# A hybrid decoder layer: q, k and the MLP's input transposed by VectorE and DMA, and every projection with the activations as the stationary operand

## The chip, the cores and the metric

The kernel runs on one core of a Trainium2 chip. The metric is the device time of one execution in microseconds. TensorE is called PE, VectorE DVE, ScalarE ACT, GpSimd POOL and SyncE SP in the profile; SP does no arithmetic here and issues the transfers (DMAs).

## The reference

One decoder layer on 256 tokens of width 2048, all in float32:

```python
h = rmsnorm(x, ln1);  dq, dk, dv, sq, sk, sv = split(h @ w_in)      # six parts of 1024 columns
# group A, 8 heads: two 64-dim maps each, partial rotary on q and k
w = softmax(q1 k1^T / 8) - lam * softmax(q2 k2^T / 8)               # causal
diff = rmsnorm(w @ dv) * (1 - lam_init)
# group B, 8 heads of 128: stick-breaking attention
z = sq sk^T / sqrt(128)
a = exp(log_sigmoid(z) + reversed exclusive cumsum of log_sigmoid(-z))   # strictly causal
sb = rmsnorm(a @ sv)
x = x + concat(diff, sb) @ w_out
x = x + square(relu(rmsnorm(x, ln2) @ w_mlp_in)) @ w_mlp_out        # 8192 wide
out = rmsnorm(x, ln_f)
```

## The kernel before

Every large product is computed to float32 accuracy from float32r operands: each operand is split into a high part (`wh`, `a[:, 0]`) and a rest (`wl`, `a[:, 1]`), and three products (high x high, high x rest, rest x high) are added in PSUM. Weights come in chunks of 512 x 512 (1 MB, `issue_dma`, SP's queue, three buffers before the MLP and six in it). A chunk is two **jobs**; for each, `issue_conv` splits a tile of 128 x 1024: ACT makes `wh` (line 214), DVE makes `wl` by a subtraction (line 217). The conversions run three jobs ahead of the products (`AHEAD`), five in the MLP.

Two forms of product stand side by side. In `products_acc` (lines 248 to 261) the activations are stationary, the weights move, 512 columns at a time, and the result has tokens on partitions: a job has 2 contraction tiles x 2 token tiles x 3 products, 12 of 512 columns. In `products_T` (lines 264 to 288), used for sq and sk alone, the weights are stationary and the result comes out transposed, with features on partitions, as attention wants its q and k: a job has 8 products of 512 columns (high and rest of the activations side by side, line 271) and 8 of 256 columns (line 276).

What products_acc makes for q and k of the differential group (dq, dk) is transposed on PE against an identity matrix (line 425, 8 transposes of 128 x 128 per block of 512 columns, in two groups of four), and so is the MLP's input x after the output projection (line 643, four per pair of tiles). For sq and sk the scale 1/rms of each token has to lie along the columns: `x_norm` builds it with one product (line 363).

The MLP's hidden layer is already transposed in another way (`turn_task`): DVE transposes 32 x 32 blocks out of PSUM into `bl` (line 711), 16 DMAs of 32 KB, all issued by SP (line 716), move the blocks to their partitions in `hT`, DVE squares the ReLU (line 718), and ACT and DVE split the result into `aT` (lines 724, 725).

The work between the products hangs on **side tasks**: generators that advance by one step, up to the next `yield`, after each job (`tick`; the first two tasks of the queue get a step). `prep_task` makes q and k ready, `diff_task` and `sb_task` are the two attentions, one per group of four heads, and end in `mixT`, the eight pairs of tiles that the output projection reads; `x2_task` makes `xs2`, the MLP's input, from x after the output projection's column block. The order of the output jobs is written out: first the tiles that are ready early for column blocks 0 and 1 (12 jobs, from `n_proj` to `n_out0`), then the last chunk of both, then blocks 2 and 3. The MLP goes in four quarters of 2048 hidden columns: four `in_group`s, then four `out_group`s that read `aT` in the order in which it was made. Within these rules a planner orders the instructions of each engine when the program is built, by times of its own; each engine then takes them in that order.

Of the kernel before, what the change touches and what calls it, by code (L numbers as in the profile page):

```python
# [18 lines left out]
P = 128  # L19
# [6 lines left out]
CK = 4  # L26
# [18 lines left out]
def tile_hybrid_layer(  # L45
# [187 lines left out]
    def run_jobs(upto, nside=2):  # L233
        while state["job"] < upto:
            i = state["job"]
            if i in hooks:
                hooks[i]()
            while state["conv"] < min(i + 1 + state["ahead"], len(jobs)):
                issue_conv()
            c, h, products, after, _ = jobs[i]  # L240
            products(h, *sp.pop(i, (None, None)))
            if after is not None:
                after()
            tick(nside)
            state["job"] += 1


    def products_acc(get_acc, act, k0, first, last):
# [12 lines left out]
        return f  # L261


    def products_T(get_acc, act, k0, done):
        def f(h, wh, wl):
            acc = get_acc()
            last = k0 + (h + 1) * HK == KT

            def high(i, j):
                kt = k0 + h * HK + j  # L270
                nc.tensor.matmul(acc[i], wh[:, j, i * P:(i + 1) * P], act(kt).rearrange("p a s -> p (a s)"),  # L271
                                 start=kt == 0, stop=False, skip_group_check=True)

            def low(i, j):
                kt = k0 + h * HK + j
                state["mm"] = nc.tensor.matmul(acc[i][:, S:2 * S], wl[:, j, i * P:(i + 1) * P], act(kt)[:, 0, :],  # L276
                                               start=False, stop=kt == KT - 1, skip_group_check=True)


            tiles = range(NB // P)  # L280
            for part in ([(i,) for i in tiles] if last else [tiles]):
                for one in (high, low):
                    for i in part:
                        for j in range(HK):
                            one(i, j)
                if last:
                    done(part[0])
        return f
# [41 lines left out]
    rstd_row = {k: cpool.tile([P, S], F32, name=f"rstd_row_{k}") for k in ("sq", "sk")}  # L330
# [20 lines left out]
    def x_norm():  # L351
# [7 lines left out]
        dg = ap_.tile([P, NT, P], F32, tag="on", name="rstd_diag", bufs=1)  # L359
        for t in range(NT):  # L360
            nc.vector.tensor_scalar_mul(dg[:, t, :], ident, rstd1[:, t:t + 1])
        rp = ps_sc.tile([P, S], F32, tag="sc", name="rstd_row_ps")
        nc.tensor.matmul(rp, negone, dg.rearrange("p t s -> p (t s)"), start=True, stop=True)
        nc.vector.tensor_scalar_mul(rstd_row["sk"], rp, -1.0)
        nc.vector.tensor_scalar_mul(rstd_row["sq"], rp, -(128.0 ** -0.5))
# [33 lines left out]

    grp = {}  # L400

    def prep_task(kind):

        src = grp[kind, "src"]
        v = src.rearrange("p t (g c) -> p t g c", c=64)
# [12 lines left out]
        yield  # L418
        dst = ap_.tile([P, HG, S], F32, tag="qkT", name=f"T_{kind}", bufs=4)
        for hp in range(HG // 2):  # L420
            tp = ps_tp.tile([P, 2 * S], F32, tag="tp", name=f"tp_{kind}_{hp}")
            for hh in range(2):
                h = hp * 2 + hh
                for t in range(NT):
                    nc.tensor.transpose(tp[:, hh * S + t * P:hh * S + (t + 1) * P],
                                        src[:, t, h * P:(h + 1) * P], ident)
            yield
            nc.vector.tensor_copy(dst[:, hp * 2:hp * 2 + 2, :],
                                  tp.rearrange("p (h s) -> p h s", h=2))
        grp[kind] = dst  # L430
# [20 lines left out]
    def diff_task(gi):  # L451
# [4 lines left out]
        for h in range(HG):  # L456
# [16 lines left out]
            e = ap_.tile([P, 2, 3 * P], F32, tag="e", name=f"e_{nm}", bufs=3)  # L473
# [37 lines left out]
    def sb_task(gi):  # L511
# [4 lines left out]
        for hp in range(HG // 2):  # L516
# [12 lines left out]
            t = ap_.tile([P, 2, 3 * P], F32, tag="e", name=f"t_{nm}", bufs=3)  # L529
# [18 lines left out]
            a = ap_.tile([P, 2, 3 * P], F32, tag="e", name=f"a_{nm}", bufs=3)  # L548
# [15 lines left out]
    def proj_T_block(kind):  # L564

        c0 = cols[kind[:2]] + int(kind[2]) * NB
        acc = {}
        dst = {}

        def get_acc():  # L570
            if not acc:
                for i in range(HG):
                    acc[i] = ps_acc.tile([P, NB], F32, tag="acc", name=f"acc_{kind}{i}")
                dst[0] = ap_.tile([P, HG, S], F32, tag="qkT", name=f"T_{kind}", bufs=4)
            return acc

        def done(i):
            t1 = ap_.tile([P, S], F32, tag="t1", name=f"t1_{kind}{i}", bufs=1)
            nc.scalar.copy(t1, acc[i][:, S:2 * S])
            nc.vector.tensor_tensor(t1, acc[i][:, 0:S], t1, op=ALU.add)  # L580
            nc.vector.tensor_tensor(dst[0][:, i, :], t1, rstd_row[kind[:2]], op=ALU.mult)

        def after():
            grp[kind] = dst[0]
            if kind[1] == "k":
                side.append(sb_task(int(kind[2])))

        for c in range(KT // CK):
# [79 lines left out]
    for nb in (0, 1):  # L668
        out_chunk(nb, KT // CK - 1)
# [275 lines left out]
```

## Time and profile before

| | us |
|---|---|
| three runs | 1119.19, 1118.60, 1118.12 (median 1118.6) |
| profiled execution | 1118.63 |
| its span (first to last instruction) | 1116.9 |
| PE busy in the span | 1106.0 |
| DVE, ACT, POOL busy | 652.8, 512.4, 2.9 |

The span is what the profile shows; the time of an execution has 1.7 us beside it. A product's duration in the profile (389 ns for 512 columns) is from its start to the end of its drain; products overlap, so the price of one in a row of them is the distance of two starts, or its piece in the chain of waits.

### The profile page before, as it was taken

How to read it: one execution, taken by the hardware profiler on the slowest of the kernel's cores; microseconds unless marked ns; L12 is line 12 of the kernel's file. 1: busy time of each engine (PE TensorE's matmuls, PEld its weight loads, DVE VectorE, ACT ScalarE, POOL GpSimd, SP SyncE). 2: the span in 40 equal slices, each digit the busy share in tenths (PEclk: the TensorE clock that was granted, in tenths of full speed). 3: DMA queues.
4: the chain of work that ended last, by engine and by line, in shares of the span. 5: the costliest groups of instructions: out<-in, count | busy, mean ns of one | idle time of the engine just before them, and what ended most of it. 6: DMA issues, size and time to landing. Idle time of an engine off the chain costs nothing.

```text
span 1116.9 us, 13378 instructions
## 1 busy us (share of the span) xinstructions
PE 1106.0 (99%) x5213; PEld 919.6 (82%) x5213; DVE 652.8 (58%) x817; ACT 512.4 (46%) x665; POOL 2.9 (0%) x16
## 2 busy tenths in 40 slices
PE   9999999999999999999999999999999999999996
PEld 6887888888888888888888888888888888888886
DVE  5755756766555655665455565545556555555752
ACT  5645544655555644444333444434444433444541
POOL 1000000000000000000000000000000000000000
PEclk9999999999999999999999999999999999999999
DMA  8754554454545854766665576666557666565712
GB/s 287 227 171 153 170 175 144 152 187 149 177 165 212 321 183 137 263 226 206 211 198 162 182 261 225 201 197 198 184 182 251 221 195 195 198 210 180 263 39 76
DMA packets 125683, 216.02 MB, mean 193 GB/s; under 512 B 8210, under 2 KB 25652, under 8 KB 125492
## 3 DMA queue, kind: packets, MB, share of 16 engines
q1 hardware_dynamic: 125332, 214.65, 57.5%
q8 instruction: 41, 0.67, 0.2%
q10 hardware_dynamic: 288, 0.52, 0.1%
q14 instruction: 22, 0.18, 0.0%
HBM read 204.65 MB, written 2.10 MB: 185 GB/s over the span
## 4 chain that ended last, share of the span: by engine, by line
PE 99%; DMA 0%; DVE 0%; SPq 0%; ACT 0%; issue 0%; DVEq 0%; ACTq 0%
PE ia L260 10%; PE ia L259 10%; PE ia L258 10%; PE ma L258 10%; PE ma L259 10%; PE ma L260 10%; PE acc_sk L271 3%; PE acc_sq L271 3%; PE oacc L260 3%; PE oacc L258 3%; PE oacc L259 3%; PE acc_dq L258 1%; PE acc_sq L276 1%; PE acc_sk L276 1%; PE acc_dk L258 1%; PE acc_dq L260 1%
## 5 line engine op out<-in xcount | busy, mean ns | idle before, releaser
L217 DVE TENSOR_TENSOR wl<-w,wh 128x1024 fp32r<-128x1024 f32 (+1 forms) x385 | 469.3, 1222 | 382.2 <-ACT wh L214 380.8
L214 ACT CAST wh<-w 128x1024 fp32r<-128x1024 f32 (+1 forms) x385 | 402.5, 1049 | 497.3 <-PE ia L260 195.7
L258 PE MATMUL ia<-wh,xs 128*128 128x512 f32 x512 | 199.4, 389 | 0.0
L260 PE MATMUL ia<-wh,xs 128*128 128x512 f32 x512 | 199.3, 389 | 0.0
L259 PE MATMUL ia<-wl,xs 128*128 128x512 f32 x512 | 199.2, 389 | 0.0
L258 PE MATMUL ma<-wh,aT 128*128 128x512 f32 x480 | 186.7, 389 | 0.0
L259 PE MATMUL ma<-wl,aT 128*128 128x512 f32 x480 | 186.7, 389 | 0.0
L260 PE MATMUL ma<-wh,aT 128*128 128x512 f32 x480 | 185.4, 389 | 0.0
L258 PEld LDWEIGHTS ia<-wh,xs 128*128 128x128 f32 x512 | 96.1, 188 | 20.0
L259 PEld LDWEIGHTS ia<-wl,xs 128*128 128x128 f32 x512 | 96.1, 188 | 19.9
L260 PEld LDWEIGHTS ia<-wh,xs 128*128 128x128 f32 x512 | 96.1, 188 | 19.9
L258 PEld LDWEIGHTS ma<-wh,aT 128*128 128x128 f32 x480 | 90.1, 188 | 18.7
L260 PEld LDWEIGHTS ma<-wh,aT 128*128 128x128 f32 x480 | 90.1, 188 | 18.7
L259 PEld LDWEIGHTS ma<-wl,aT 128*128 128x128 f32 x480 | 90.1, 188 | 18.7
L258 PE MATMUL oacc<-wh,mixT 128*128 128x512 f32 x128 | 50.5, 394 | 0.0
L259 PE MATMUL oacc<-wl,mixT 128*128 128x512 f32 x128 | 50.1, 391 | 0.0
L260 PE MATMUL oacc<-wh,mixT 128*128 128x512 f32 x128 | 49.8, 393 | 0.0
L271 PE MATMUL acc_sk<-xs,wh 128*128 128x512 f32 x128 | 36.7, 399 | 0.0
L271 PE MATMUL acc_sq<-xs,wh 128*128 128x512 f32 x128 | 34.9, 397 | 0.0
L260 PEld LDWEIGHTS oacc<-wh,mixT 128*128 128x128 f32 x128 | 24.0, 188 | 4.9
L258 PEld LDWEIGHTS oacc<-wh,mixT 128*128 128x128 f32 x128 | 24.1, 188 | 4.8
L259 PEld LDWEIGHTS oacc<-wl,mixT 128*128 128x128 f32 x128 | 24.1, 188 | 4.8
(224 smaller groups left out, 1105.6 us busy)
## 6 DMA issues: line engine op xcount, KB each, us to landing
w<-in_w_mlp_in_dram SPq DMA_DIRECT2D x64, 1024.0 KB, 5.7
w<-in_w_mlp_out_dram SPq DMA_DIRECT2D x64, 1024.0 KB, 7.3
w<-in_w_in_dram SPq DMA_DIRECT2D x46, 1024.0 KB, 5.2
w<-in_w_out_dram SPq DMA_DIRECT2D x16, 1024.0 KB, 5.1
hT<-bl SPq DMA_DIRECT2D x256, 32.0 KB, 1.9
w<-in_w_in_dram SPq DMA_DIRECT2D x4, 512.0 KB, 7.8
x<-in_x_dram SPq DMA_DIRECT2D x3, 512.0 KB, 10.1
lnf_t<-in_ln_f_dram SPq DMA_DIRECT2D x1, 1024.0 KB, 6.5
```

The lines of the kernel that those rows point to most:

```text
L214: state["wh"] = nc.scalar.copy(wh[:, j], w[:, j])
L217: state["wl"] = nc.vector.tensor_tensor(wl[:, j], w[:, j], wh[:, j].bitcast(F32), op=ALU.subtract)
L258: nc.tensor.matmul(acc[t], a[:, 0, st], wh[:, j, :], start=s0, stop=False)
L259: nc.tensor.matmul(acc[t], a[:, 0, st], wl[:, j, :], start=False, stop=False)
L260: state["mm"] = nc.tensor.matmul(acc[t], a[:, 1, st], wh[:, j, :], start=False, stop=s1)
L271: nc.tensor.matmul(acc[i], wh[:, j, i * P:(i + 1) * P], act(kt).rearrange("p a s -> p (a s)"), start=kt == 0, stop=False, skip_group_check ...
L276: state["mm"] = nc.tensor.matmul(acc[i][:, S:2 * S], wl[:, j, i * P:(i + 1) * P], act(kt)[:, 0, :], start=False, stop=kt == KT - 1, skip_g ...
```

## The change

All six projections use `products_acc`; `products_T` and `proj_T_block` go. What is made with tokens on partitions (dq, dk, sq, sk, and the MLP's input x) is transposed as the MLP's hidden layer is, by a common function `turn`: two DVE transposes and 16 DMAs, which now alternate between SP's and GpSimd's queue (in the MLP's hidden layer too). For q and k the DMAs land in the tile that the projection wrote (`src`), and ACT copies from there to the order that attention reads. `prep_task` takes six steps where it took four, for sq and sk too. In the 12 output jobs before `n_out0` tasks get two steps each. One pair of output jobs is exchanged. The tag "e" (exponentials) has two buffers, no longer three.

```diff
@@ run_jobs
             tick(nside)
+            if n_proj <= i < n_out0:
+                tick(nside)
@@ products_T: removed
-                nc.tensor.matmul(acc[i], wh[:, j, i * P:(i + 1) * P], act(kt).rearrange("p a s -> p (a s)"),
-                                 start=kt == 0, stop=False, skip_group_check=True)
...
-                state["mm"] = nc.tensor.matmul(acc[i][:, S:2 * S], wl[:, j, i * P:(i + 1) * P], act(kt)[:, 0, :],
...
@@ x_norm
-        rp = ps_sc.tile([P, S], F32, tag="sc", name="rstd_row_ps")
-        nc.tensor.matmul(rp, negone, dg.rearrange("p t s -> p (t s)"), start=True, stop=True)
...
+        nc.vector.tensor_scalar_mul(rstd_sq, rstd1, 128.0 ** -0.5)
@@ new
+    def turn(dst, bl, src, engines):
+        for t in range(NT):
+            nc.vector.transpose(bl[:, t].rearrange("p f (k b) -> p f k b", b=32),
+                                src[t].rearrange("p (k f a) -> p f k a", k=4, f=4))
+        dv = dst.rearrange("p (t i) k b -> p t i (k b)", t=NT)
+        for i in range(4):
+            for f in range(4):
+                engines[(i * 4 + f) % len(engines)].dma_start(
+                    dv[f * 32:(f + 1) * 32, :, i, :], bl[i * 32:(i + 1) * 32, :, f, :])
@@ prep_task
+        if kind[0] == "d":
+            rotary(kind, src)
+        yield
+        bl = ap_.tile([P, NT, 4, 4 * 32], F32, tag="bl", name=f"bl_{kind}", bufs=1)
+        turned = src.rearrange("p t c -> p (t c)").rearrange("p (i k b) -> p i k b", k=HG, b=32)
+        turn(turned, bl, [src[:, t, :] for t in range(NT)], [nc.gpsimd, nc.sync])
+        for _ in range(4):
+            yield
+        dst = ap_.tile([P, HG, S], F32, tag="qkT", name=f"T_{kind}", bufs=4)
+        nc.scalar.copy(dst.rearrange("p k (i b) -> p k i b", b=32), turned.rearrange("p i k b -> p k i b"))
...
-                    nc.tensor.transpose(tp[:, hh * S + t * P:hh * S + (t + 1) * P],
-                                        src[:, t, h * P:(h + 1) * P], ident)
-            yield
-            nc.vector.tensor_copy(dst[:, hp * 2:hp * 2 + 2, :],
-                                  tp.rearrange("p (h s) -> p h s", h=2))
@@ diff_task, sb_task: three tiles of tag "e"
-            e = ap_.tile([P, 2, 3 * P], F32, tag="e", name=f"e_{nm}", bufs=3)
+            e = ap_.tile([P, 2, 3 * P], F32, tag="e", name=f"e_{nm}", bufs=2)
...
@@ proj_T_block: removed; proj_block appends prep_task for q and k of both groups, sb_task behind sk
-            nc.scalar.copy(t1, acc[i][:, S:2 * S])
-            nc.vector.tensor_tensor(t1, acc[i][:, 0:S], t1, op=ALU.add)
-            nc.vector.tensor_tensor(dst[0][:, i, :], t1, rstd_row[kind[:2]], op=ALU.mult)
...
@@ x2_task
+        turn(x2T, bl, [xt[nb][:, t, :] for t in range(NT)], [nc.sync, nc.gpsimd])
+        yield
+        yield
         for p2 in range(nb * 2, nb * 2 + 2):
-                    nc.tensor.transpose(tp[:, j * S + t * P:j * S + (t + 1) * P],
-                                        xt[nb][:, t, (kt % 4) * P:(kt % 4 + 1) * P], ident)
...
+                nc.scalar.activation(hi[j], x2T[:, :, k, :], AF.Copy, scale=g)
...
+                nc.vector.scalar_tensor_tensor(lo[j], x2T[:, :, k, :], g, hi[j].bitcast(F32),
+                                               op0=ALU.mult, op1=ALU.subtract)
+            yield
@@ output jobs
+    jobs[n_out0 + 1], jobs[n_out0 + 2] = jobs[n_out0 + 2], jobs[n_out0 + 1]
@@ turn_task of the MLP
-                    nc.sync.dma_start(hv[f * 32:(f + 1) * 32, :, i, :], bl[i * 32:(i + 1) * 32, :, f, :])
+            turn(hT, bl, [acc[t] for t in range(NT)], [nc.sync, nc.gpsimd])
```

## Rows read from the trace of the kernel before

**Rows 1.** The page's first part: busy us, share of the span, instructions of each engine.
```profile
PE 1106.0 (99%) x5213; PEld 919.6 (82%) x5213; DVE 652.8 (58%) x817; ACT 512.4 (46%) x665; POOL 2.9 (0%) x16
```
**Rows 2.** The page's second part: granted clock of PE, tenths, in 40 slices.
```profile
PEclk9999999999999999999999999999999999999999
```
**Rows 3.** The waits of PE: total us, times, longest; the first of three.
```profile
PE warm_a L321 <- DVE three_c L105: 1.3, 1, 1.3
```
**Rows 4.** The waits of all engines, the second longest in total.
```profile
ACT wh L214 <- PE ia L260: 195.7, 126, 1.9
```
**Rows 5.** The chain of waits between 157 and 289 us, shares by line.
```profile
by line: PE acc_sk L271 22.7%; PE acc_sq L271 22.5%; PE acc_sq L276 11.5%; PE acc_sk L276 11.5%; PE acc_sv L258 5.7%; PE acc_sv L260 5.5%; PE acc_sv L259 5.5%; PE sc_d L467 2.6%; PE sc_s L524 2.0%; PE o_d L508 2.0%; PE o_s L508 2.0%; PE wtp
```
**Rows 6.** The chain in order of time, 244 to 262 us: start, us, what.
```profile
247.57 1.84 PE acc_sq L271 x8
249.41 0.95 PE acc_sq L276 x8
```
**Rows 7.** Timeline of PE in the MLP: start, duration; 11 products stand between.
```profile
459.73 0.39 PE L258 MATMUL ia<-wh,xs 128*128 128x512 f32 x1
...
462.45 0.39 PE L258 MATMUL ia<-wh,xs 128*128 128x512 f32 x1
```
**Rows 8.** The chain in order of time, two stretches (48 to 75, 359 to 425 us).
```profile
49.32 0.43 PE rstd_row_ps L363 x2
...
64.99 0.44 PE tp_dk L425 x4
...
373.98 0.44 PE x2tp L643 x4
```
**Rows 9.** Groups of instructions by line: count, busy us, mean ns, idle before.
```profile
L217 DVE TENSOR_TENSOR wl<-w,wh 128x1024 fp32r<-128x1024 f32 (+1 forms) x385 | 469.3, 1222 | 382.2 <-ACT wh L214 380.8
...
L711 DVE STREAM_TRANSPOSE bl<-ia 128x512 f32<-128x512 f32 x32 | 20.9, 692 | 0.0
...
L580 DVE TENSOR_TENSOR t_sk<-acc_sk,t_sk 128x256 f32<-128x256 f32 x8 | 3.4, 420 | 1.5 <-ACT t_sk L579 1.5
...
L579 ACT COPY t_sq<-acc_sq 128x256 f32<-128x256 f32 x8 | 3.0, 375 | 3.4 <-DVE T_sq L581 1.5 <-PE acc_sq L271 1.0 <-PE acc_sq L276 0.8
...
L608 ACT ACTIVATE src_dk<-acc_dk,rstd 128x512 f32<-128x512 f32 x4 | 2.7, 689 | 2.8 <-PE acc_dk L260 2.7
```
**Rows 10.** Instructions on hT (ns min/median/max), and the page's DMA issues (us to landing).
```profile
L716 SPq DMA_DIRECT2D hT<-bl x256: 585/595/1825, 433.6 to 1031.2; - x128
...
hT<-bl SPq DMA_DIRECT2D x256, 32.0 KB, 1.9
```
**Rows 11.** Timeline of all engines at the end of the first quarter's last in_group.
```profile
498.90 10.92 SPq L716 DMA_DIRECT2D hT<-bl  x16
...
511.15 1.23 DVE L718 SCALAR_TENSOR_TENSOR hT<-hT 128x1024 f32<-128x1024 f32 x1
...
513.84 1.29 DVE L725 TENSOR_TENSOR aT<-hT,aT 128x512 fp32r<-128x512 f32 x2
...
514.59 0.39 PE L260 MATMUL ma<-wh,aT 128*128 128x512 f32 x1
```
**Rows 12.** The page's DMA issues: count, KB each, median us to landing.
```profile
w<-in_w_in_dram SPq DMA_DIRECT2D x46, 1024.0 KB, 5.2
```
**Rows 13.** Instructions on the weight tile w: SP's longest issue.
```profile
L195 SPq DMA_DIRECT2D w<-in_w_out_dram x16: 367/368/2333, 291.0 to 364.9; - x16
```
**Rows 14.** Timeline at the end of the output projection.
```profile
409.51 1.28 DVE L652 TENSOR_TENSOR x<-x,oacc 128x512 f32<-128x512 f32 x2
...
409.80 0.39 PE L258 MATMUL ia<-wh,xs 128*128 128x512 f32 x1
```
**Rows 15.** Chain and timeline around the second stick-breaking group.
```profile
288.60 0.23 PE acc_sk L276 x2
...
292.86 0.67 PE sc_s L524 x6
...
357.10 0.74 DVE L157 SCALAR_TENSOR_TENSOR mixT<-mtp_s,g2T,mixT 128x512 fp32r<-128x512 f32 x1
```

More of the change, by code (lines that the diff above doesn't have):

```diff
@@ L260, in f @@
                     state["mm"] = nc.tensor.matmul(acc[t], a[:, 1, st], wh[:, j, :], start=False, stop=s1)
[L261 to L270, printed above, removed]
-                nc.tensor.matmul(acc[i], wh[:, j, i * P:(i + 1) * P], act(kt).rearrange("p a s -> p (a s)"),
-                                 start=kt == 0, stop=False, skip_group_check=True)
-            def low(i, j):
-                kt = k0 + h * HK + j
-                state["mm"] = nc.tensor.matmul(acc[i][:, S:2 * S], wl[:, j, i * P:(i + 1) * P], act(kt)[:, 0, :],
[L277 to L287, printed above, removed]
         return f
@@ L329, in tile_hybrid_layer @@
     rstd_dq = cpool.tile([P, NT], F32, name="rstd_dq")
-    rstd_row = {k: cpool.tile([P, S], F32, name=f"rstd_row_{k}") for k in ("sq", "sk")}
+    rstd_sq = cpool.tile([P, NT], F32, name="rstd_sq")
     def sumsq(dst, src, name):
@@ L404, in prep_task, with rotary @@
         src = grp[kind, "src"]
+        if kind[0] == "d":
[8 more added lines that the diff above has]
+        nc.scalar.copy(dst.rearrange("p k (i b) -> p k i b", b=32), turned.rearrange("p i k b -> p k i b"))
+        grp[kind] = dst
+    def rotary(kind, src):
         v = src.rearrange("p t (g c) -> p t g c", c=64)
@@ L528, in sb_task @@
             z = sc[:, :, :3 * P]
-            t = ap_.tile([P, 2, 3 * P], F32, tag="e", name=f"t_{nm}", bufs=3)
+            t = ap_.tile([P, 2, 3 * P], F32, tag="e", name=f"t_{nm}", bufs=2)
             nc.scalar.activation(t, z, AF.Abs)
@@ L547, in sb_task @@
             yield
-            a = ap_.tile([P, 2, 3 * P], F32, tag="e", name=f"a_{nm}", bufs=3)
+            a = ap_.tile([P, 2, 3 * P], F32, tag="e", name=f"a_{nm}", bufs=2)
             nc.scalar.activation(a, z, AF.Exp)
@@ L562, in tile_hybrid_layer @@
     order = [f"{k}{g}" for g2 in ("d", "s") for g in range(2) for k in (g2 + "q", g2 + "k", g2 + "v")]
[L564 to L578, printed above, removed]
-            nc.scalar.copy(t1, acc[i][:, S:2 * S])
-            nc.vector.tensor_tensor(t1, acc[i][:, 0:S], t1, op=ALU.add)
-            nc.vector.tensor_tensor(dst[0][:, i, :], t1, rstd_row[kind[:2]], op=ALU.mult)
[L583 to L588, printed above, removed]
-            view = w_in[0, c * CK * P:(c + 1) * CK * P, c0:c0 + NB].rearrange("(k p) n -> p k n", p=P)
-            add_chunk(view, products_T(get_acc, act_xs, c * CK, done), after if c == KT // CK - 1 else None)
     def proj_block(kind):
@@ L605, in after @@
                            bufs=2)
-            sc_ = rstd_dq if kind[1] == "q" else rstd1
+            sc_ = {"dq": rstd_dq, "sq": rstd_sq}.get(kind[:2], rstd1)
             for t in range(NT):
@@ L613, in after @@
                 side.append(diff_task(int(kind[2])))
+            if kind[:2] == "sk":
+                side.append(sb_task(int(kind[2])))
         for c in range(KT // CK):
@@ L620, in tile_hybrid_layer @@
     for kind in order:
-        (proj_T_block if kind[:2] in ("sq", "sk") else proj_block)(kind)
+        proj_block(kind)
     n_proj = len(jobs)
```

32 lines of the change are left out of this document (8 added, 24 removed).

## The prediction, made before the change was run

> **What bounds the kernel now.** I read the engine totals first: the reader is to see PE at 99% of the span with no other engine over 58% [rows 1]. A busy PE could still be a slow one, so the clock row is next: the granted clock is in its top tenth in all 40 slices, the upper of its two levels (2.4 GHz), so nothing is to be won or lost by a faster clock [rows 2]. Then the waits of PE: three in the whole execution, 1.9 us together, all before 8 us, of which the longest is shown [rows 3]. PE therefore has its operands on time from beginning to end, and the span is a sum of PE instructions. The waits of the other engines say the same from their side: ScalarE's conversions of weights sit idle until PE gives a buffer back [rows 4]. So two questions decide: how many microseconds of PE work the change takes away, and whether the new route delivers every transposed tile before PE comes to it.
>
> **PE work that goes: the four sq and sk blocks.** Between 157 and 289 us the chain of waits is all PE, and its shares give the old form its price: 22.7 and 22.5% for the 512-column products, twice 11.5% for the 256-column ones, together 68.2% of 132 us, 90.0 us [rows 5]. In the undisturbed stretch one job of this form (8 and 8 products) is 1.84 + 0.95 = 2.79 us [rows 6]. The new form needs for the same job 12 products of 512 columns. In the MLP 12 such starts lie 462.45 - 459.73 = 2.72 us apart, 0.2267 us each [rows 7]. There are 4 blocks of 8 jobs, 384 products: 87.1 us. Saved 2.9 us by the totals, 32 x 0.07 = 2.2 us by the clean jobs; the totals also hold the jobs that attention work interrupts, and the new form will be interrupted too, so I take 2.8. The number of columns is the same in both forms; what goes is a per-instruction loss, 0.1186 us for 256 columns against half of 0.2267.
>
> **PE work that goes: transposes.** Four of them take 0.44 us of the chain, both for q and k and for the MLP's input [rows 8]. By the code q and k of the differential group lose 8 such groups, the MLP's input 8 more: 16 x 0.44 = 7.0 us. The product that spreads rstd over columns goes too: 0.43 us [rows 8]. Nothing is added on PE: sq and sk take the new route as well. Sum on PE: 2.8 + 7.0 + 0.4 = 10.2 us.
>
> **What VectorE and ScalarE get.** Twelve turns (8 of q and k, 4 of the MLP's input) cost two 128x512 transposes each, 0.69 us by the ones in the trace (these read PSUM, the new ones SBUF; I take the same): 16.6 us more. Eight 128x512 copies out of PSUM (at the same 0.69), 16 additions and 16 multiplications of 0.42 go from VectorE: 19 us less. ScalarE loses 16 copies of 0.375 (6.0 us), and gets 8 evictions of 0.69 and 8 copies of 128x1024, for which I take two evictions each: 10.6 us more [rows 9]. Both stay far below PE, and conversions run ahead of PE as far as the buffers go, so all this costs nothing as long as that cover of some jobs (2.72 us each) holds. The splits of the MLP's input keep their number. Fewer buffers for the exponentials (two for three) cost nothing either: within a task only two are alive. If two tasks collide, the softmax is late next, not PE.
>
> **What the queues get.** Each turn issues 16 transfers of 32 KB. SP issues one in 0.595 us and it lands 1.9 us after the issue began [rows 10]; a whole turn of the MLP takes SP 10.92 us, 0.68 each [rows 11]. The change adds 192 transfers and gives half of all 448 to GpSimd: SP goes from 256 to 224, and 5.5 us per turn instead of 10.9. In the projections this is new work in front of the weight loads: eight turns of 5.5 us. A chunk of weights lasts two jobs, 5.4 us, and there are three buffers: a load is issued when a buffer's second half is converted and its own first half is converted five jobs later, 13.6 us, of which it needs 5.2 to land [rows 12] and 5.5 for the turn: 2.9 us are left, and the conversions' lead of three jobs behind them. Nothing for this, 0 to 1 us per turn as the upper end.
>
> **The unknown: an issue by GpSimd.** No row of before has one. Bounds: not below SP's 0.595 us for the same transfer, above by the longest SP issue of any kind, 2.33 us [rows 10, 13]. The nearest row is the same transfer on SP, so I take a value near 0.7, and look for the point from which it matters. Call the issue p. At each quarter's end, the last group's turn has to be done when the output product reaches it. SP's first issue comes at 498.90, the squared ReLU at 511.15, the second halves of the operand from 513.84 on, and PE uses the first of them at 514.59 without a visible wait: there is no slack to lend [rows 11]. Eight issues of GpSimd are as long as today's sixteen of SP when p = 10.92 / 8 = 1.37 us. The last quarter of the MLP's input is the other deadline: its last product ends and the first MLP product starts at 409.80, the residual addition is done at 410.8 [rows 14], two transposes and one subtraction in between bring 413.4, then 8p, 1.3 us from the end of an issue to its landing, and half a microsecond for the first split: 415.2 + 8p, wanted after 12 tiles of 6 x 0.2267 us, at 426.1. Again p = 1.37. So below 1.37 us nothing is late, and above it five places (four quarters and this one) lose 8 x (p - 1.37) each, 40 x (p - 1.37) in all, if the order on PE is not laid out for it.
>
> The Trainium skill (DMA: Bandwidth & Descriptors, section Latency and other measured facts) gives about 0.6 us to the first byte on SP's path and about 1 us on GpSimd's; with 1 us for an issue, which is an estimate from that page, nothing would be late either. No row here shows it.
>
> **The longer way to the second stick-breaking group.** Today sk's last product ends at 288.8 and the first scores run from 292.9 [rows 15]. After the change: eviction 1.4, transposes 1.4 with a subtraction of 1.2 before them, 8p, landing 1.3, copy 1.4: 6.7 + 8p, 12.3 us at p = 0.7, so 8 us later than now. What this delays is the last pair of the mixed heads, ready at 357.8 today [rows 15]. By the code the last step of its task comes 20 jobs after sk's block now and 15 after the change (two steps per job in the twelve output jobs), so it is today's pacing and not the latency that makes it late, and 13 us of pacing go. The exchange of two output jobs lets both columns use the next-to-last pair first, 2.7 us more. Cost nothing; it starts to cost when 2.7 + 8p comes to 13.6 + 2.7, at p = 1.7.
>
> **Sum.** 1118.6 - 10.2 = 1108.4 us. The profiled execution took 1118.6, its span 1116.9; the median of the runs is 1118.6 as well, so no correction is needed.
>
> **Rivals.**
> *Some turns are late, but not all.* p between 1.37 and 1.55, or the order planned for PE is a little wrong in places: 2 to 7 us come back, 1111 to 1116. For it: the quarter's end has no slack [rows 11]. Against it: SP's half is done 5 us earlier than now. Chance 0.14.
>
> *Nothing is won.* The freed time goes into waits for weights: eight turns on SP's queue, where a turn waits for VectorE in front of the next load, at 1.2 us each eat 10 us: about 1118. Against it the 2.9 us worked out above and the lead behind them. It also stands for a gain and a loss that happen to cancel. Chance 0.08.
>
> *GpSimd's issue is slow, slower than before.* One mechanism: VectorE's instructions hold each issue up. Its commonest takes 1.22 us [rows 9] and VectorE is busy 58% of the time; an issue that waits for a whole one takes 0.68 + 1.22 = 1.9 us, a turn 15 us, and five places lose 4.2 us each: 21 us, 1108.4 + 21 = 1129.6. It decides from p = 1.37 + 10.2 / 40 = 1.62; at the upper bound of 2.33 it would be 1147. For it: GpSimd is idle today after its masks, so nothing shows how it lives beside VectorE [rows 1]. Against it: the transfer is small and regular. Chance 0.15.
>
> The Trainium skill speaks for a part of this rival (SBUF — State Buffer, section Who interferes with whom): GpSimd cannot write its descriptors while VectorE runs a copy or a scalar operation in a mode that takes both ports, but a two-tensor operation leaves the write side free. By that rule the 1.22 us subtraction [rows 9], two tensors, would hold nothing up, and the forecast stands; no run here shows it yet.
>
> **How the numbers follow.** The forecast itself (nothing late) has 0.63; its own range is 1107 to 1111, from 2.2 to 2.9 us for the blocks and a late last quarter of some 2 us. A measurement of this kernel tells 0.2%, 2.2 us, from no change: 1116.4 to 1120.8 counts as same. Faster: 0.63 + 0.14 = 0.77; same 0.08; slower 0.15. A range of 1106.5 to 1117.5 holds the first two cases and part of the third; left out is the slow issue and a little below.
>
> **What would show it.** PE busy falls by about 10 us while the sum of its idle time stays under 3 us; products of sq and sk 0.227 us apart; no PE transposes of src or x; GpSimd's issues near 0.7 us, in any case below 1.37; the squared ReLU at a quarter's end starts no later after its transposes than today's 12 us. The prediction is wrong if PE waits for xs, aT or the scores' operands, which would stand in the waits of PE, or if waits for weights appear in the projections.

## The result, and the profile after

| | before | after |
|---|---|---|
| median of the runs, us | 1118.69 (4 runs) | 1110.37 (4 runs, 1109.93 to 1112.65) |
| profiled execution / its span, us | 1118.63 / 1116.9 | 1109.93 / 1108.2 |
| first product of the MLP's first layer starts at | 409.80 [rows 14] | 402.43 |
| from there to the end of the span | 707.1 | 705.8 |

The ratio of after to before is 0.993, with an interval of 0.9913 to 0.9947: 8.3 us faster by the medians, where 10.2 were forecast. (The ratio compares means, by which it is 7.8 us.) The time lies inside the range, 2 us above the forecast. Of the 8.7 us by which the span is shorter, 7.4 are there before the MLP begins.

The page of the changed kernel, the lines that answer [rows 1, 2]:

```profile
PE 1095.4 (99%) x5019; PEld 905.7 (82%) x5019; DVE 647.8 (58%) x798; ACT 519.4 (47%) x665; POOL 121.0 (11%) x240
PEclk9999999999999999999999999999999999999999
```

TensorE is busy for 10.6 us less than before, still 99% of a shorter span, at the upper clock level throughout. That figure must not be read as the forecast 10.2 come true: e6, e7 and e12 below, with the same 5019 products, are busy for 1096.2 to 1097.0 us, so it is uncertain by 1.6 us. Its waits (total us, times, longest), as in [rows 3]:

```profile
PE oacc L260 <- ACT mixT L156: 1.3, 1, 1.3
PE warm_a L296 <- DVE three_c L105: 1.3, 1, 1.3
PE xtp L319 <- DMA x<-in_x_dram: 1.2, 1, 1.2
PE ps_g1T L284 <- DMA rows<-in_ln_dram: 0.4, 1, 0.4
```

Three of them belong to the first microseconds, as before; the one for x varies from nothing to 1.2 us between the runs. Together they are 4.2 us, where the prediction wanted less than 3. The first is new: a product of the output projection waits for the last pair of the mixed heads. The timeline of TensorE and ScalarE there (start, duration, engine and line; in brackets the idle time before it and what ended it):

```profile
351.45 0.60 PE L428 MATMUL mtp_s<-ident,on_s 128*128 128x128 f32 x4
...
352.61 0.68 ACT L156 ACTIVATE mixT<-mtp_s,g2T 128x512 fp32r<-128x512 f32 x1
...
353.34 0.50 PE L260 MATMUL oacc<-wh,mixT 128*128 128x512 f32 x1 [1.28 <-ACT mixT L156]
```

Between the last transposes of the stick-breaking group and the product that reads them there is nothing left for TensorE to do; before the change 11 other products stood there:

```profile
354.90 0.60 PE L446 MATMUL mtp_s<-ident,on_s 128*128 128x128 f32 x4
...
357.88 0.39 PE L258 MATMUL oacc<-wh,mixT 128*128 128x512 f32 x1
```

The four sq and sk blocks, by the shares of the chain of waits between 153 and 283 us, as in [rows 5]:

```profile
by line: PE acc_sk L260 11.6%; PE acc_sq L260 11.5%; PE acc_sk L261 11.3%; PE acc_sq L262 11.2%; PE acc_sq L261 11.2%; PE acc_sk L262 11.2%; PE acc_sv L260 5.8%; PE acc_sv L262 5.6%; PE acc_sv L261 5.6%; PE sc_d L449 2.9%; PE sc_s L506 2.1%
```

The six sq and sk shares make 68.0% of 130 us, 88.4 us, against 90.0 by the same reading before: 1.6 us, good to some 0.3 us, since the shares are rounded. Summed over both traces as distances from one start to the next, the products of sq and sk take 89.4 us in place of 91.3: 1.9 us.

GpSimd's issues and VectorE's transposes, which no row of before had: first the tile's own view (shortest, median, longest in ns), then groups of instructions.

```profile
L378 SPq DMA_DIRECT2D hT<-bl x128: 585/595/1937, 440.6 to 1017.3; - x128
L378 POOL DMA_DIRECT2D hT<-bl x128: 533/533/550, 441.5 to 1017.1; - x128
```

```profile
L373 DVE STREAM_TRANSPOSE x2bl<-x 128x512 f32<-128x512 f32 x8 | 5.3, 691 | 0.0
```

An issue by GpSimd takes 0.533 us at the median and 0.550 at most here (0.674 once, for a tile of dq), less than SyncE's 0.595. The median time from issue to landing, by tile and queue:

```profile
hT<-bl SPq DMA_DIRECT2D x128, 32.0 KB, 1.9
hT<-bl POOLq DMA_DIRECT2D x128, 32.0 KB, 1.8
x2T<-x2bl POOLq DMA_DIRECT2D x32, 32.0 KB, 2.8
...
src_sk<-bl_sk SPq DMA_DIRECT2D x16, 32.0 KB, 4.5
```

So a turn of the second stick-breaking group's keys takes 9.6 us from its first issue (284.48) to its last landing (294.08). Its issues alone take 6.1 us, GpSimd's half 4.2.

### The profile page after: what moved, and what is told of

It reads as the page before. It is cut to its first block, busy times and chain, and to the rows that moved or that the text cites. A ratio compares the mean times of both kernels' runs of the same rounds, so it can differ in the third digit from the quotient of the medians.

```text
span 1108.2 us, 13750 instructions
## 1 busy us (share of the span) xinstructions
PE 1095.4 (99%) x5019; PEld 905.7 (82%) x5019; DVE 647.8 (58%) x798; ACT 519.4 (47%) x665; POOL 121.0 (11%) x240
## 4 chain that ended last, share of the span: by engine, by line
PE 98%; DMA 0%; DVE 0%; ACT 0%; SPq 0%; issue 0%; DVEq 0%; ACTq 0%
PE ia L260 10%; PE ia L262 10%; PE ia L261 10%; PE ma L261 10%; PE ma L262 10%; PE ma L260 10%; PE oacc L260 3%; PE oacc L262 3%; PE oacc L261 3%; PE acc_dk L260 1%; PE acc_dq L261 1%; PE acc_sk L260 1%; PE acc_sq L260 1%; PE acc_dq L262 1%; PE acc_sk L261 1%; PE acc_dq L260 1%
## 5 line engine op out<-in xcount | busy, mean ns | idle before, releaser
L217 DVE TENSOR_TENSOR wl<-w,wh 128x1024 fp32r<-128x1024 f32 (+1 forms) x385 | 468.7, 1221 | 393.7 <-ACT wh L214 392.7
L378 POOL DMA_DIRECT2D hT<-bl x128 | 67.4, 535 | 529.9 <-DMA w<-in_w_mlp_in_dram 244.3
L378 POOL DMA_DIRECT2D x2T<-x2bl x32 | 16.8, 534 | 114.6 <-DVE x L615 72.7
```

The source lines that it names most:

```text
L217: state["wl"] = nc.vector.tensor_tensor(wl[:, j], w[:, j], wh[:, j].bitcast(F32), op=ALU.subtract)
L378: engines[(i * 4 + f) % len(engines)].dma_start(dv[f * 32:(f + 1) * 32, :, i, :], bl[i * 32:(i + 1) * 32, :, f, :])
```

## Experiments

Each kernel is the changed kernel with one edit (e11 is e5 with one more). The table gives the median, the ratio to the kernel before that ran beside it on the same chip (changed kernel: 0.993), the start of the MLP's first product, and the rest of the profiled span after it (changed kernel: 402.43 and 705.8).

| run | median, us | ratio, interval | MLP starts | rest |
|---|---|---|---|---|
| e1: all turns by SyncE | 1119.9 | 1.0008, 0.9999 to 1.0016 | 404.60 | 715.1 |
| e2: MLP's input on TensorE | 1115.45 | 0.9965, 0.9952 to 0.9979 | 405.71 | 707.2 |
| e3: dq, dk on TensorE | 1114.87 | 0.9963, 0.9950 to 0.9975 | 409.26 | 705.8 |
| e4: sq, sk in the old form | 1112.7 | 0.9941, 0.9929 to 0.9954 | 404.76 | 705.9 |
| e5: MLP's input by SyncE | 1119.5 | 1.0004, 0.9995 to 1.0013 | 402.87 | 713.5 |
| e6: all but MLP's input by SyncE | 1110.61 | 0.9920, 0.9907 to 0.9934 | 402.30 | 705.8 |
| e7: fills on GpSimd | 1110.52 | 0.9920, 0.9907 to 0.9934 | 402.87 | 705.7 |
| e8: last keys on TensorE | 1111.23 | 0.9924, 0.9912 to 0.9937 | 402.41 | 706.1 |
| e9: slow issue, MLP's input | 1130.85 | 1.0096, 1.0082 to 1.0110 | 402.94 | 726.5 |
| e10: slow issue, hidden tiles | 1188.94 | 1.0621, 1.0606 to 1.0635 | 402.70 | 784.9 |
| e11: SyncE, second buffers | 1120.37 | 1.0008, 0.9999 to 1.0017 | 403.38 | 714.3 |
| e12: three queues for sq, sk | 1109.66 | 0.9913, 0.9899 to 0.9926 | 401.60 | 706.2 |

The start of the MLP also carries what the first 20 us lost, ahead of anything that an edit changes: the first product for dk starts at 32.6 and 32.8 us in e1 and e3, and between 30.2 and 30.8 in the changed kernel and in e2, e4, e6 and e12.

### What each part is worth: e2, e3, e4

Each puts one part of the work back on TensorE, with the code of the kernel before.

```diff
 # e2, x2_task
-        turn(x2T, bl, [xt[nb][:, t, :] for t in range(NT)], [nc.sync, nc.gpsimd])
...
+            tp = ps_tp.tile([P, HK * S], F32, tag="tp", name=f"x2tp{p2}")
...
+                    nc.tensor.transpose(tp[:, j * S + t * P:j * S + (t + 1) * P],
+                                        xt[nb][:, t, (kt % 4) * P:(kt % 4 + 1) * P], ident)
...
+            split_pair(xs2[p2], tp, gT[2][:, p2 * HK:(p2 + 1) * HK], True)
```

> Only the MLP's input is transposed on PE again (32 transposes); q and k and the projections stay changed. Theory: these cost their price on PE, 32 x 0.109 = 3.5 us: 1113.9 (1113 to 1114.8). Rival (they were hidden, or the new route of this part costs as much in waits): 1110 to 1111.5.

Measured: the ratio is 0.0035 higher, 3.9 us; the median lies above the expected 1113 to 1114.8. The start of the MLP moves by 3.3 us, the rest of the span by 1.4. As distances between starts, the 32 transposes take 2.7 us in this trace, and the products of the output projection and of the MLP's first layer, which they interrupt, 1.3 us more than in the changed kernel.

```diff
 # e3, prep_task
+        if kind[0] == "d":
...
+                        nc.tensor.transpose(tp[:, hh * S + t * P:hh * S + (t + 1) * P],
+                                            src[:, t, h * P:(h + 1) * P], ident)
+                yield
+                nc.vector.tensor_copy(dst[:, hp * 2:hp * 2 + 2, :],
+                                      tp.rearrange("p (h s) -> p h s", h=2))
+            grp[kind] = dst
+            return
```

> Only q and k of the differential group are transposed on PE again (32 transposes). Theory: 3.5 us on PE: 1113.9 (1113 to 1114.8). Rival (hidden, or the longer route made attention products collide): 1110 to 1111.5.

Measured: 0.0033 higher, 3.7 us; the median lies just above the expected 1114.8. (Its profiled execution is the slowest of its runs, 1116.8, so its start of the MLP overstates the cost.)

```diff
 # e4
+        nc.tensor.matmul(rp, negone, dg.rearrange("p t s -> p (t s)"), start=True, stop=True)
...
-        proj_block(kind)
+        (proj_T_block if kind[:2] in ("sq", "sk") else proj_block)(kind)
```

> Only sq and sk are made with the weights stationary again, with the row of rstd they need; the rest stays changed. Theory from the two traces (blocks worth 1.6 us, the row 0.4, but PE's wait of 1.3 us for the last pair of mixed heads goes): about 1111 (1110 to 1112). Rival (the prediction's 2.8 + 0.4, wait an accident): 1113.6 (1113 to 1114.5).

Measured: 0.0011 higher, 1.2 us. The median, 1112.7, lies between the two ranges expected (1110 to 1112, 1113 to 1114.5). The wait for mixT is gone; all waits of TensorE are those of the first microseconds:

```profile
PE warm_a L322 <- DVE three_c L105: 1.3, 1, 1.3
PE ps_g1T L310 <- DMA rows<-in_ln_dram: 0.4, 1, 0.4
PE xtp L345 <- DMA x<-in_x_dram: 0.4, 1, 0.4
```

The three undoings make 3.9 + 3.7 + 1.2 = 8.8 us, against 7.8 by the changed kernel's own ratio (0.007 x 1119). Each interval is about 1.5 us to either side, the changed kernel's 1.9, so a part is good to some 2 us. How much they are depends on that kernel's ratio, which one run of 1112.65 raises: against e6 and e7 (0.992), where TensorE has the same products, they are 5.0, 4.8 and 2.3 us, more than the whole. So the times agree with the 3.5 forecast for each set of transposes and don't fix it. The sq and sk blocks bring 1.2 to 2.3 net, which can't tell 2.8 + 0.4 less the wait of 1.3 from 1.6 + 0.4 less that wait; only the readings in the traces, 1.6 and 1.9, speak for the smaller price. No run undoes the second step per job, the exchange of the output jobs or the two buffers of tag "e" by itself.

### Whether the route's speed matters, and where: e1, e5, e6

```diff
 # e1
-        turn(turned, bl, [src[:, t, :] for t in range(NT)], [nc.gpsimd, nc.sync])
+        turn(turned, bl, [src[:, t, :] for t in range(NT)], [nc.sync])
-        turn(x2T, bl, [xt[nb][:, t, :] for t in range(NT)], [nc.sync, nc.gpsimd])
+        turn(x2T, bl, [xt[nb][:, t, :] for t in range(NT)], [nc.sync])
-            turn(hT, bl, [acc[t] for t in range(NT)], [nc.sync, nc.gpsimd])
+            turn(hT, bl, [acc[t] for t in range(NT)], [nc.sync])
```

> All turns are issued by SP again, 16 issues each; nothing by GpSimd. Theory (PE work is the time, the route's speed matters only where PE waits): a turn takes SP 10.9 us where it takes 5.5 now, but only the end of the second stick-breaking group has no cover; 1110.4 us as with both queues, up to 2 us more there (1110 to 1112.5). Rival (the prediction's deadlines are hard, GpSimd's half is needed): PE waits at the MLP input's last quarter and in the quarters, 5 us or more: over 1115.

Measured: the whole gain is gone, and the theory's 1110 to 1112.5 is missed. With SyncE alone a turn is not hidden everywhere. Of the five deadlines that the prediction had named, the four quarter ends show no wait; the fifth does, the last quarter of the MLP's input. TensorE's longest waits of e1:

```profile
PE ia L260 <- ACT xs L605: 5.8, 2, 5.0
PE oacc L260 <- ACT mixT L156: 1.3, 1, 1.3
```

The next two runs divide this edit: e5 has only its second pair of lines, the MLP's input by SyncE; e6 only the first and the third.

```diff
 # e5
-        turn(x2T, bl, [xt[nb][:, t, :] for t in range(NT)], [nc.sync, nc.gpsimd])
+        turn(x2T, bl, [xt[nb][:, t, :] for t in range(NT)], [nc.sync])
```

> All 32 transfers of each turn of the MLP's input by SyncE; the turns of q, k and of the MLP's hidden tiles keep GpSimd's half. Theory A (of the five turns that follow straight on one another after the attention, only those of the MLP's input are short of time, and GpSimd's half is worth its 8.7 us there alone): as slow as with every turn on SyncE, 1118 to 1120 us, with one wait of TensorE of about 5 us near 434 us of the span, behind the splits of the MLP's input. Rival B (the hidden tiles' turns are what lost the time, by holding the queue before the MLP's input or at the quarter ends): stays at 1110 to 1112 us.

> The mirror of the run before: the turns of q, k and of the hidden tiles by SyncE alone, only the MLP's input keeps GpSimd's half. Theory A: 1110 to 1111.5 us, no wait over 2 us in TensorE and none at the quarter ends. Rival B: 1118 to 1120 us. By the prediction's quarter-end bound (SyncE alone, as it is before the change, already costs nothing there): same as A.

A turn has 16 transfers, not the 32 named for e5. Measured: the four turns of the MLP's input, 32 of GpSimd's 224 transfers, carry all of it. e5 is as slow as e1; e6 is as fast as the changed kernel, although its turns of q and k take 11 to 14 us each, and those of the hidden tiles 11 to 15. The timeline of the last quarter of the MLP's input, in the changed kernel:

```profile
402.14 1.28 DVE L615 TENSOR_TENSOR x<-x,oacc 128x512 f32<-128x512 f32 x2
...
413.02 1.30 DVE L373 STREAM_TRANSPOSE x2bl<-x 128x512 f32<-128x512 f32 x2
...
415.90 5.08 SPq L378 DMA_DIRECT2D x2T<-x2bl  x8
...
428.06 1.71 ACT L605 ACTIVATE xs<-x2T,g2T 128x256 fp32r<-128x256 f32 x4
429.33 1.67 DVE L608 SCALAR_TENSOR_TENSOR xs<-x2T,g2T,xs 128x256 fp32r<-128x256 f32 x4
```

and in e5 (VectorE, SyncE, TensorE):

```profile
413.82 1.30 DVE L373 STREAM_TRANSPOSE x2bl<-x 128x512 f32<-128x512 f32 x2 [5.79 <-DMA x2T<-x2bl]
...
416.73 6.90 DVE L217 TENSOR_TENSOR wl<-w,wh 128x1024 fp32r<-128x1024 f32 x6
431.37 1.68 DVE L608 SCALAR_TENSOR_TENSOR xs<-x2T,g2T,xs 128x256 fp32r<-128x256 f32 x4 [7.74 <-ACT xs L605]
...
416.84 12.64 SPq L378 DMA_DIRECT2D x2T<-x2bl  x16
...
431.38 0.50 PE L260 MATMUL ia<-wh,xs 128*128 128x512 f32 x1 [4.37 <-ACT xs L605]
```

The addition of the residual is done at 403.4, but the transposes follow it only at 413.0. With both queues the transfers have landed at 423.4, and the splits come at 428.1, in their own place on ScalarE, with no wait of TensorE. With SyncE alone VectorE stands 5.79 us in front of the last quarter's transposes, until the third turn's transfers are done; the last transfer of all is issued by 429.5 and has landed by 430.75; ScalarE and VectorE stand in front of the splits and convert no weights meanwhile (7.74 us of idle time on VectorE), and TensorE waits 4.4 us. The clock is the rest of the loss: after the wait it is for some microseconds at the lower of its two levels (0.50, 1.2 GHz; 1.00 is the upper, 2.4 GHz). The windows of e5 show length, busy us and count of each engine, mean granted clock, DMA share and GB/s.

```profile
430.00:436.00 6.00, 4.62 (x13) 3.70 (x14) 4.04 (x6) 3.59 (x6) 0.00 (x0) 0.72 0.90 294
436.00:440.00 4.00, 4.00 (x19) 3.28 (x19) 2.45 (x3) 2.06 (x2) 0.00 (x0) 1.00 1.05 407
```

In the changed kernel the same stretch shows 29 products in place of 13, at 1.00.

### Why the last quarter starts late: e11

Theory after e5: the four turns share one pair of buffers, and the last one waits for the third to give it back. Here SyncE alone issues as in e5, and the second and fourth turn get a pair of their own.

```diff
+        if nb % 2:
+            both = mlp["sb"].tile([P, D], F32, tag="lnf", name=f"x2both{nb}", bufs=1)
+            x2T = both[:, :NB * NT].rearrange("p (i k b) -> p i k b", k=4, b=32)
+            bl = both[:, NB * NT:].rearrange("p (t f c) -> p t f c", t=NT, f=4)
...
-        turn(x2T, bl, [xt[nb][:, t, :] for t in range(NT)], [nc.sync, nc.gpsimd])
+        turn(x2T, bl, [xt[nb][:, t, :] for t in range(NT)], [nc.sync])
...
+        if nb == 3:
+            mlp["lnf"] = mlp["sb"].tile([P, D], F32, tag="lnf", name="lnf_t", bufs=1)
+            nc.sync.dma_start(mlp["lnf"], ln_f.partition_broadcast(P))
```

> SyncE alone turns the MLP's input, as in the run that lost 8.7 us, but the second and fourth turn have a pair of buffers of their own (the space of the final norm's weights, which are loaded after them). Theory A (what is lost is the time that the fourth turn waits for the third's buffers, 403.4 to 415.9 us; SyncE is fast enough otherwise): 1110 to 1111.5 us and no wait near 431 us. Rival E (16 transfers of 0.65 to 0.8 us on one queue are too slow in themselves here): 1117 to 1120 us, the wait stays.

Measured: 1120.37, and TensorE waits 6.7 us at the same place. Buffers alone don't bring the time back. SyncE and VectorE around the third and fourth turn:

```profile
388.44 18.25 SPq L378 DMA_DIRECT2D x2T<-x2bl  x16
...
408.73 1.68 DVE L613 SCALAR_TENSOR_TENSOR xs<-x2T,g2T,xs 128x256 fp32r<-128x256 f32 x4 [8.29 <-ACT xs L610]
...
412.02 1.28 DVE L623 TENSOR_TENSOR x<-x,oacc 128x512 f32<-128x512 f32 x2
```

The second turn now starts earlier, but the third takes SyncE 18.25 us, and VectorE stands 8.29 us in front of the third turn's splits. The residual addition of the fourth, free to run at about 403, is behind them in VectorE's order and comes at 412.0. So the rival holds: 16 issues on SyncE alone are too slow in this stretch. In e5 the delay was handed on by the buffer (the 5.79 us above); with that tie gone the order on VectorE hands it on. No run changes that order, so this last step is read from the trace and not tested.

### From which issue time it matters: e7, e9, e10

e7 put six fills ahead of each of GpSimd's transfers.

```diff
 # e7, turn
+                if eng is nc.gpsimd:
+                    for _ in range(6):
+                        nc.gpsimd.memset(slowt, 0.0)
```

> Six fills of a 128x128 tile (0.204 us each in the first rows of GpSimd) stand ahead of each of GpSimd's transfers, so that one of them goes out each 1.76 us in place of 0.53. The prediction's price: five turns are late by 16 x (1.76 - 1.37) = 6.2 us each, less what the neighbouring work covers as it took it, 40 x (1.76 - 1.37) = 15.6 us: about 1126 us, with a wait of TensorE at every one of the four quarter ends. Theory A (only the turns of the MLP's input are short of time, the quarter ends not): a wait after the attention larger than the 5 us of SyncE alone, 1118 to 1124 us, and none or little at the quarter ends.

It tests nothing of this. The fills depend on nothing, so they were placed far ahead of the transfers; src_dq's eight issues by GpSimd are over at 51.1 us as in the changed kernel (50.9). It shows only that 277 us of fills on GpSimd cost nothing:

```profile
L382 POOL MEMSET slowt<- 128x128 f32 x1344 | 277.4, 206 | 76.1
```

e9 and e10 use copies that read the tile being turned, chained to the transfers.

```diff
 # e9 (slow = 3, MLP's input), e10 (slow = 4, hidden tiles), turn
...
+                        if state.get("pool"):
+                            st.enter_context(tc.issue_after(state["pool"].ins))
+                        for _ in range(slow):
+                            c = nc.gpsimd.tensor_copy(slowt, bl[:, 0, 0, :])
+                        st.enter_context(tc.issue_after(c.ins))
...
```

> Three copies of a 128x128 tile by GpSimd, which read the tile that is being turned, stand ahead of each of its transfers of the MLP's input (and only there), chained so that they can't run ahead; at the 0.284 us of the first rows' copy, one transfer goes out each 0.53 + 0.86 = 1.39 us. The prediction's break-even (1.37): nothing lost, 1110 to 1111 us. Theory A in its present form: the four turns share one pair of buffers, the last can't start before 415.9 us of the span whatever the residual does (its addition is done at 403.4), and it then lands 415.9 + 8 x 1.39 + 2 = 429 us in place of 423.4, when the splits that were done at 428.1 to 431.0 without a wait need it: a wait of TensorE of 1 to 4 us near 430 us and 1112 to 1117 us.

> Four such copies ahead of each of GpSimd's transfers of the hidden tiles (and only there): one goes out each 0.53 + 1.14 = 1.67 us, so a turn takes 8 x 1.67 + 1.9 = 15.3 us from its first issue to its last landing. The prediction's price for the four quarter ends: 32 x (1.67 - 1.37) = 9.6 us, about 1120 us. Theory A (one pair of buffers ties the four turns of a quarter together; a turn's cycle of 15.3 + 4.8 us is longer than the 16.4 us in which the groups follow one another, so the turns fall further behind from group to group): the fourth starts about 6 us later and takes 8 us longer than now, about 10 us over what the quarter end hides; four quarters, 1125 to 1150 us, with waits of TensorE for aT at each.

The copies took longer than expected (first e9, then e10):

```profile
L385 POOL CAST slowt<-x2bl 128x128 bf16<-128x128 f32 x96 | 45.7, 476 | 97.2 <-DMA w<-in_w_out_dram 70.0 <-DVE x2bl L374 23.2
```

```profile
L385 POOL CAST slowt<-bl 128x128 bf16<-128x128 f32 x512 | 252.7, 494 | 371.4 <-DVE bl L374 347.2
```

So p was 0.533 + 3 x 0.476 = 1.96 us in e9 and 0.533 + 4 x 0.494 = 2.51 us in e10. (The starts of GpSimd's issues lie 2.06 and 2.62 us apart on average.) By the prediction's price e9 should lose 8 x (1.96 - 1.37) = 4.7 us and e10 32 x (2.51 - 1.37) = 36.5 us. Against e6 and e7 (1110.6) they lost 20.3 and 78.4, more than either expectation allowed (1112 to 1117, 1125 to 1150). The copies do not slow VectorE's subtractions for the weights: 1229 ns on average in e10, 1221 in the changed kernel. The longest waits of TensorE in e9 and in e10:

```profile
PE ia L261 <- ACT xs L616: 10.3, 3, 4.4
...
PE ia L263 <- DVE xs L619: 1.2, 1, 1.2
PE ia L261 <- ACT wh L215: 1.1, 1, 1.1
```

```profile
PE ma L261 <- ACT aT L693: 40.7, 6, 9.7
PE ma L261 <- ACT wh L215: 9.1, 8, 1.1
PE ma L262 <- DVE wl L218: 4.3, 8, 0.6
```

Two things make it dearer. The turns of a stretch stand one behind the other, so a longer turn delays all that follow it: in e9 the third turn's splits are late as well, and the fourth is issued from 437.5 on in place of 415.9. And after a long wait the clock is down; e9's windows, behind a wait of 4.3 us that ended at 434.8:

```profile
434.00:440.00 6.00, 5.16 (x12) 4.09 (x13) 2.92 (x6) 1.70 (x4) 3.10 (x9) 0.51 0.61 190
440.00:446.00 6.00, 6.00 (x26) 4.85 (x26) 1.22 (x1) 1.34 (x2) 5.50 (x15) 0.92 0.22 54
```

Of e10's 78.4 us the waits are 54.1; TensorE's busy time is 25.9 us longer than in the changed kernel with the same 5019 instructions, since products take longer at the lower level of the clock (0.50 from 500 to 506 us, the first wait of 4.9 us having ended at 500.3).

### The new wait for mixT: e8, e12

```diff
 # e8, prep_task
+        if kind == "sk1":
...
+                        nc.tensor.transpose(tp[:, hh * S + t * P:hh * S + (t + 1) * P],
+                                            src[:, t, h * P:(h + 1) * P], ident)
...
```

> Of q and k only the keys of the second stick-breaking group are transposed by TensorE as before (two blocks of four transposes, 0.88 us), all else as in the changed kernel. Theory C (the 1.3 us wait of TensorE for the last pair of mixT comes from the longer way of these keys, through the order in which the products were then laid out): the wait goes, since 22 products stand between the last transposes of the stick-breaking group and the first product on its pair, 1.3 to 1.6 us won for 0.9 paid: 1109.4 to 1110.0 us. Rival D (the wait is of VectorE's and ScalarE's splits, late for their other work): the wait of about 1.3 us stays and the time rises to 1111.3 us.

Measured: the wait is gone, and so is its profit: 0.9 us of transposes were paid. Medians of 1111.2 here and 1110.6 and 1110.5 in e6 and e7 beside it can't be told apart; the 1109.4 to 1110.0 of the expectation is missed, while its account of the wait holds.

```diff
 # e12, prep_task
-        turn(turned, bl, [src[:, t, :] for t in range(NT)], [nc.gpsimd, nc.sync])
+        turn(turned, bl, [src[:, t, :] for t in range(NT)],
+             [nc.gpsimd, nc.sync, nc.scalar] if kind[0] == "s" else [nc.gpsimd, nc.sync])
```

> The turns of the stick-breaking q and k go out on three queues, ScalarE's beside GpSimd's and SyncE's; nothing else is changed. With 6 transfers in a row in place of 8 the keys are ready about 2 us earlier, and 11 products stand between the last transposes of the stick-breaking group and the first product on its pair of mixT. Theory C (the 1.3 us wait comes from the longer way of the keys): the wait is gone, no product of TensorE is added, 1108.8 to 1109.8 us. Rival: ScalarE's 5 issues of about 0.6 us delay its splits of the weights or the keys' scaling as much: wait or time as before, 1110 to 1111 us.

Measured: the wait is gone with no work added to TensorE: its waits are again those of the first microseconds alone. Its MLP starts 0.8 us earlier than in the changed kernel (402.43):

```profile
401.60 0.39 PE L260 MATMUL ia<-wh,xs 128*128 128x512 f32 x1
```

The median, 1109.66, is the lowest of all kernels here, 0.9 below e6 and e7; the intervals overlap, so by time alone it is not established that it beats the changed kernel. Its span, 1107.8, is 9.1 us shorter than the kernel's before.

## Why the prediction was right, point by point

*TensorE bounds the kernel, and what goes from it is the gain.* Right: 99% before and after, and the gain is the products and transposes removed, less one wait.

*Transposes, 7.0 us.* Right as far as the runs resolve it: e2 and e3 give back 3.9 and 3.7, forecast 3.5 each, with 2 us of doubt in either.

*The sq and sk blocks, 2.8 us.* Mis-sized: 1.6 us by the chain's shares, 1.9 by the distances of starts. The prediction knew that attention work interrupts both forms, and still took a value near the totals' 2.9, with 87.1 us for the new form from uninterrupted products; the interrupted ones make it 88.4.

*The longer way to the second stick-breaking group costs nothing.* This step failed, for a small price. It held today's pacing to be what makes the last pair late, let the change bring the last step from 20 jobs behind sk's block to 15, and gave the latency 13 us of room, up to p = 1.7. With p at 0.533 TensorE still waits 1.3 us. Counted in large products (12 to a job), TensorE's order has 264 of them between the last of sk and the last transposes, and 253 before: not 5 jobs fewer, but the 11 products more that used to cover the way to the reader. The pacing did give: 185 products from the scores to the transposes, before 236. The longer way took more: the scores stand 79 products behind sk, before 17.

```profile
294.85 1.05 ACT L396 COPY T_sk<-src_sk 128x1024 f32<-128x1024 f32 x1
...
300.87 0.83 PE L506 MATMUL sc_s<-T_sq,T_sk 128*128 128x128 f32 x6
```

The last product of sk ends at 283.0, so the keys are ready 12.9 us behind it, where the prediction's 6.7 + 8p gives 11.0: transfers of these tiles land 3.8 to 4.5 us after their issue, not 1.9. The scores run 17.9 us behind it (before: 3.9), since their place in TensorE's order lies 5 us behind the keys. e12, e8 and e4 shorten this way in three manners: 253, 242 and 226 products to the last transposes, and no wait in any of them.

*Sum.* With these terms: 7.0 + 1.6 + 0.4 - 1.3 = 7.7 us, against 8.3 measured. Without the wait it is 9.0, and e12, which has none, is 9.1 us shorter than the kernel before by its span. The range, 11 us wide, would have held the time with either size of the blocks; that it came out right says little about this term.

*VectorE, ScalarE, the loads of weights cost nothing.* Right as to time: no wait of TensorE for weights with q and k turned by both queues, and one of 0.2 us with SyncE alone (e6). The rival in which eight turns hold up the loads, at 1.2 us each, is excluded by e6, where they take up to twice as long.

*GpSimd's issue.* Taken at 0.7, measured at 0.533, below the bound of 0.595 that the prediction took from SyncE. The rival in which VectorE holds each issue up did not appear: 533 ns shortest and median, 550 longest for the hidden tiles, with VectorE busy 58% of the time. By the rule that the prediction cited from the Trainium skill (SBUF — State Buffer, section Who interferes with whom) two-tensor operations would not hold an issue up, and this trace agrees.

*Nothing is late below p = 1.37, and above it five places lose 8 us per microsecond each.* Not decisive here, but wrong in the dates behind it and in price. For the MLP's input the prediction let the last quarter's transfers start 3.6 us after the MLP's first product (413.4 - 409.8); in the changed kernel they start 13.5 us after it (415.9 - 402.4), held back by VectorE's order (the transposes at 413.0, the third turn's splits up to 415.9). It had them wanted 16.3 us after it; the splits run 25.6 us after it, and TensorE waits for nothing. The two errors cancel at GpSimd's real speed, which is luck. In e5 the last turn takes 13.9 us from first issue to last landing, as long as one by both queues would at p = 1.58 (8 x 1.58 + 1.3); the loss was 8.9 us (against e6) where the prediction's price gives 8 x (1.58 - 1.37) = 1.7. For the quarter ends, SyncE alone costs nothing, as the prediction read from [rows 11]; with p = 2.51 they cost twice its price (e10). The true break-even for the MLP's input lies between a last turn of 7.5 us (no loss) and one of 13.9; where exactly was not tried.

## What to carry to other kernels

Work taken from a bounding engine comes back at its full price only if nothing that it moves arrives later than the place which the fixed order gives it; count the products that stand between the last producer and its first reader, and when that count falls to zero, expect a wait. An engine's fixed order can put a product later than its operands need: here 5 us of the delay were of that kind. A deadline is best read in the trace as the time at which the consumer in order stands there, and checked by slowing one route alone; a chain of turns hands its delay on, and a wait of TensorE here cost about half as much again through the clock. Half of the issues on a second queue was worth about 9 us at one place, the MLP's input, and nothing at the other turns.

## What the runs showed of the hardware

- GpSimd issues a 32 KB transfer between tiles faster than SyncE: 0.533 against 0.595 us, with little scatter (533 to 550 ns over 128 issues). From issue to landing it was 1.8 us for GpSimd and 1.9 for SyncE on the hidden tiles. The Trainium skill (DMA: Bandwidth & Descriptors, section Latency and other measured facts) gives about 1 us to the first byte for GpSimd's path and 0.6 for SyncE's; that difference does not show here.
- Two queues don't always halve a turn: the keys of the second stick-breaking group took 9.6 us with both and 12.4 with SyncE alone (e6). With both, the median transfer of sk's tiles landed 3.8 us (GpSimd) to 4.5 us (SyncE) after its issue, with SyncE alone 1.9.
- Beside VectorE's operations with two inputs in SBUF, GpSimd's copies slow down; its issues do not, and its fills hardly. The copies of e9, shortest, median and longest in ns:

```profile
L385 POOL CAST slowt<-x2bl x96: 289/295/1364, 359.4 to 451.5; 128x128 bf16<-128x128 f32 x96
```

  In e10 all 273 copies with no VectorE instruction beside them took 293 to 303 ns, and the 20 beside a transpose alone, which reads PSUM, 291 to 297; the 183 beside a subtraction for the weights alone had a median of 1163. The 1344 fills of e7 took 206 ns on average. This is what the Trainium skill says (SBUF — State Buffer, section Who interferes with whom): a VectorE instruction with two SBUF inputs contends with a GpSimd instruction that reads SBUF, and not with one that only writes it.
- In e1, e5, e9, e10 and e11 each wait of TensorE of 4.2 us or more was followed by a stretch at the lower level of its clock: over the six microseconds behind the wait the mean granted clock was 0.50 to 0.72. After the wait of 1.3 us for mixT and three of 1.1 to 1.5 us in e9 it stayed at 1.00; of eight waits of 1.1 us in e10 two were followed by 0.72.
